# A hybrid decoder layer in float32 on TensorE: loads two tiles ahead, a fifth weight buffer, another place for the embedding's split

## The chip, the core and the metric

The kernel runs on one core of a Trainium2 chip. The metric is the device time of one execution in microseconds: the median of three runs of the kernel before, 2093.87 (2093.08 to 2097.32). All times of single instructions come from one further execution that the hardware profiler recorded.

## The reference

One layer of a decoder trunk in float32 on x of 1024 tokens x 2048 channels:

```python
h = rmsnorm(x, g_pre)
u = h @ w_in                     # 2048 x 7184, split into the heads' inputs and two gates
o_gla = rmsnorm(gla_chunked(...)) * silu(g_gate)    # 4 heads, gated linear attention
o_sb = stick_breaking(...) * silu(s_gate)           # 8 heads, stick-breaking attention
x = x + rmsnorm(concat(o_gla, o_sb) @ w_out, g_post)
x = x + sigmoid(x @ w_ple_gate + b) * (p @ w_ple_proj)
```

p has 256 channels for each token; `p @ w_ple_proj` is called the embedding here, and `w_p` is its weight.

## The kernel before

**Arithmetic.** A float32 operand is used as a sum of two rounded parts. `split(hi, lo, src)` makes them: ScalarE copies `src` into `hi` (L113), VectorE subtracts `hi` from `src` into `lo` (L114). A product in float32 is three matmuls for each 128 x 128 block of weight: hi with hi, lo with hi, hi with lo. Matmuls are 128 x 128 by 512 tokens; the tokens are in two halves (`hf` 0 and 1).

**Blocks.** The three big square products (gates, w_out, and w_g, which is `w_ple_gate`) are done in Strassen-Winograd form: seven products of half size instead of eight, with sums S1 to S4 of activations and differences of weights (b11, t1, t2, t3, t4). A stage is a loop over eight columns j of one or two products. A product is 24 matmuls into one `dn` bank. A stage with two products in a step loads three wide raw weights (`wload2`, 512 KB, 128 x 1024) in each step, takes differences of them on VectorE (`sub`, L876, `add`, L873), splits the results (`wsplit`) and, in the gates and w_out, stores two of the sums. Raw wide weights are in a pool `wr` of four buffers, the split ones in `wh` and `wl` of three each.

**The gates' S1 and S2.** They were summed from x earlier and stored in DRAM. `x_set` (L760) loads them a tile of 128 x 512 at a time (`u<-S2x_d`), and splits each (`ah<-u`, `al<-u`) into the activations of the gates' later stages. It is a generator that runs beside the small products of the gates (L818, L825; weights `raw`, `hi`, `lo`) and beside stick-breaking attention. That uses ScalarE for X<-z and E<-z (L592, L593), VectorE for a scan and copies, ScalarE again for X<-E (L333); later the rows come turned as `v`, split into `s`, and go to TensorE as t<-s,u.

**The embedding.** In three stages of w_g, products carry an `embed` between their matmuls: six matmuls with w_p into a bank z, t, z, o in turn. Its weight is loaded to `pr`, and split to `ph` and `pl` (128 x 256, one buffer each). Behind the product `gated` adds two banks (`ev<-dn,st`), ScalarE makes the sigmoid (`g<-ev,c`, L1203), VectorE multiplies it with the embedding (L1204, `ev<-t,g`).

**What sets the order.** The program is written in stages, and a scheduler puts the instructions of each engine into one list, by priority and by its own estimate of when operands are there. `tc.high_priority(offset=n)` draws the work inside it forward. `ahead` does so by 700 for wide loads and their splits, `soon` by 300 for what empties a bank; the embedding's load and split are drawn forward by 400. Each engine then works through its own list in order. The loads here are issued from SP's list.

The lines of the embedding before:

```python
wr, wh, wl = mt("pr", 1, 256), mt("ph", 1, 256, F32R), mt("pl", 1, 256, F32R)
with tc.high_priority(offset=400):
    dma2(wr, w_p[n])
    split(wh, wl, wr)
```

Of the kernel before, what the change touches and what calls it, by code (L numbers as in the profile page):

```python
# [12 lines left out]
F32R = mybir.dt.float32r  # L13
# [48 lines left out]
def layer(ctx, tc, xT, w_in, w_gate, w_lr, w_a2, b_a, g_pre, g_head, w_out, g_post,  # L62
# [4 lines left out]
    dma2 = nc.sync.dma_start  # L67
# [19 lines left out]
    def nm(base):  # L87
        serial[0] += 1
        return f"{base}_{serial[0]}"

    def ps(tag):
        bufs = {"dn": 4, "z": 2, "t": 1, "o": 1}[tag]
        return psum.tile([P, HT], F32, tag=tag, name=nm(tag), bufs=bufs)
# [6 lines left out]
    def mm(o, lhsT, rhs, start, stop):  # L100
        PE.matmul(o, lhsT, rhs, start=start, stop=stop)  # L101

    def f(t):
        return t.bitcast(F32)
# [7 lines left out]
    def split(hi, lo, src, eng=None):  # L112
        A.activation(hi, src, AF.Copy)  # L113
        (eng or V).tensor_tensor(lo, src, f(hi), op=ALU.subtract)  # L114
# [19 lines left out]
    def act_wide(hf, kp):  # L134
        return (act.tile([P, W], F32R, tag=f"h{hf}_{kp}", name=nm("ah")),
                act.tile([P, W], F32R, tag=f"l{hf}_{kp}", name=nm("al")))

    def part(t, k):
        return t[:, (k % 2) * HT:(k % 2 + 1) * HT]

    def parts(pairs):
        return [tuple(part(t, i) for t in pair) for pair in pairs for i in range(2)]
# [22 lines left out]
    pace = [0, PACE_QKV]  # L165

    def advance(queue):
        while queue:
            if next(queue[0], None) is not None:
                return True  # L170
            queue.popleft()
        return False
# [38 lines left out]
    pair = {}  # L211
# [3 lines left out]
    with tc.tile_pool(name="start", bufs=1) as sp:  # L215
# [21 lines left out]
        for q in range(4):  # L237
            w = [wload(w_in[n, q]) for n in range(2)]
            for kk in range(4):
                k = 4 * q + kk  # L240
                sl = slice(kk * P, (kk + 1) * P)
                for hf in HALVES:
                    raw = sp.tile([P, HT], F32, tag="xraw", name=nm("xraw"), bufs=20)
# [36 lines left out]
    with tc.tile_pool(name="att", bufs=1, reuse_waits="tile") as ap:  # L280
# [11 lines left out]
        def at(tag, shape=(P, HT), dt=F32):  # L292
            pool, bufs = (ap, BUFS[tag]) if tag in BUFS else (own[1], {**GLA_BUFS, **SB_BUFS}[tag])
            return pool.tile(list(shape), dt, tag=tag, name=nm(tag), bufs=bufs)
# [463 lines left out]
        g_sets = {"S1": [], "S2": []}  # L758

        def x_set(name, hf):  # L760
            for k in range(8):
                t = at("u")
                dma2(t, part(sx_d[name][k // 2], k))
                yield 1
                if k % 2 == 0:
                    wides = act_wide(hf, k // 2)
                pair = tuple(part(x, k) for x in wides)
                split(*pair, t)
                g_sets[name].append(pair)

        def small_product(a, src, evac):
            p = ps("dn")
            for q in range(2):
                hi, lo = wload(part(src, q))
                for kk in range(4):
                    k = 4 * q + kk
                    sl = slice(kk * P, (kk + 1) * P)
                    ah, al = a[k]
                    mm(p, hi[:, sl], ah, k == 0, False)
                    mm(p, lo[:, sl], ah, False, False)  # L780
                    mm(p, hi[:, sl], al, False, k == 7)
                    if k % 2:
                        step()
            with tc.high_priority(offset=300):
                evac(p)
# [22 lines left out]
        while beside:  # L808
            advance(beside)
        rate[1], pace[1] = RATE_TAIL, PACE_TAIL  # L810
        beside.append(x_set("S2", 1))
        for j in range(8):
            small_product(x_act[0][:8], w_gate[0, 0, j], keep_u1(j))
        while beside:
            advance(beside)
        beside.append(x_set("S1", 0))
        order_11 = (6, 7, 0, 1, 2, 3, 4, 5)
        for j in order_11[:8 - LAST_11]:  # L818
            small_product(x_act[0][8:], w_gate[1, 0, j], keep_11(j, lambda: at("u")))
# [9 lines left out]
    def mt(tag, bufs, n=W, dt=F32, name=None):  # L829
        pool = keep if tag == "ar" else mp if tag in ("wr", "wh", "wl", "cw") else late[0]  # L830
        return pool.tile([P, n], dt, tag=tag, name=nm(name or tag), bufs=bufs)
# [12 lines left out]
    if True:  # L844
# [31 lines left out]
            V.tensor_tensor(dst, a, b, op=ALU.subtract)  # L876

        def wload2(src):
            raw = mt("wr", 4)
            dma(raw, src)  # L880
            return raw

# [142 lines left out]
        for j in range(8):  # L1025
            with ahead():
                b11, t1, t2 = (wload2(w_gate[kh, nh, j]) for kh, nh in ((0, 0), (0, 1), (1, 1)))
                sub(t1, t1, b11)
                sub(t2, t1, t2)
                w2, w1 = wsplit(t2), wsplit(t1)  # L1030
                add(b11, b11, t2)
                dma2(t2_d[j], t2)
                dma2(t3_d[j], b11)
            p = product(g_sets["S2"], w2)
            with soon():
                add(u(j), p, part(u1_s[j // 2], j) if j < 6 else u(j))
            p = product(g_sets["S1"], w1)
            with soon():
                add(v(j), p, u(j))
# [5 lines left out]
        for j in range(8):  # L1045
            with ahead():
                t4, t2 = wload2(w_gate[1, 0, j]), wload2(t2_d[j])
                add(t4, t4, t2)
                w = wsplit(t4)
            p = product(x_act[1][8:], w)  # L1050
            with soon():
                add(u(j), p, u(j))
        drain()

        for j in range(8):
            with ahead():
                w = wsplit(wload2(t3_d[j]))
            p = product(sets["S3"], w)
            gate(j, 1, p, u(j))
            gate(8 + j, 1, p, v(j))  # L1060
# [110 lines left out]
        def load_p(hf):  # L1171
            raw = staged(pT[hf])
            hi, lo = mt("sq", 1, dt=F32R, name="ph"), mt("acc", 1, dt=F32R, name="pl")
            split(hi, lo, raw)
            p_act[hf] = parts([(hi, lo)])

        def embed(n, hf):
            def go():
                if hf not in p_act:
                    load_p(hf)  # L1180
                wr, wh, wl = mt("pr", 1, 256), mt("ph", 1, 256, F32R), mt("pl", 1, 256, F32R)
                with tc.high_priority(offset=400):
                    dma2(wr, w_p[n])
                    split(wh, wl, wr)
                z = ps(next(pw_tags))
                for k in range(2):
                    sl = slice(k * P, (k + 1) * P)
                    ah, al = p_act[hf][k]
                    mm(z, wh[:, sl], ah, k == 0, False)
                    mm(z, wl[:, sl], ah, False, False)  # L1190
                    mm(z, wh[:, sl], al, False, k == 1)
                pw[n, hf] = z
            return go

        def gated(n, hf, p, other, last=False):
# [43 lines left out]
        for j in range(8):  # L1239
            with ahead():  # L1240
                w = wsplit(wload2(w_g[1, 0, j]))
            p = product(sets[1], w, embed(j, 1))
            with soon():
                gated(j, 1, p, u(j))
# [29 lines left out]
        for j in range(8):  # L1274
            with ahead():
                w = wsplit(wload2(w_g[1, 1, j]))
            p = product(sets["S4"], w, embed(8 + j, 1))
            with soon():
                gated(8 + j, 1, p, v(j))
        drain()  # L1280

        for j in range(8):
            with ahead():
                t2, t3, t4 = wload2(t2_d[j]), wload2(w_g[0, 0, j]), wload2(w_g[1, 0, j])
                add(t3, t3, t2)
                add(t4, t4, t2)
                w3, w4 = wsplit(t3), wsplit(t4)
            p = product(sets["S3"], w3, embed(8 + j, 0), at=6 if j == 0 else 4)
            with soon():
                gated(8 + j, 0, p, v(j))  # L1290
                add(u(j), p, u(j))
            p = product(sets["A22"], w4, embed(j, 0))
            with soon():
                gated(j, 0, p, u(j), last=j >= 6)
# [74 lines left out]
```

## Time and profile before

| what | value |
|---|---|
| runs | 2093.87 us median of 3 (2093.08 to 2097.32) |
| profiled execution | 2095.95 us, of it 2094.3 span |
| TensorE busy | 2068.5 us of the span |
| VectorE, ScalarE, GpSimd busy | 1485.8, 876.8, 112.0 us |
| granted TensorE clock | 0.998 of full speed |

The span is from the first to the last instruction. The waits of an engine are the stretches in which it did nothing before an instruction, put down to what released it. A product's matmuls stand 0.227 us apart when nothing holds them up, a product takes 5.44 us and an embedding 1.36. Stages in question: S2's last tile is split at 1154 us; the gates' three-load stage runs from about 1190 to 1290, w_out's from 1440 to 1530; the embedding's first gated stage is around 1780 to 1840, the last stage from about 1980 to the end.

### The profile page before, as it was taken

Reading aid. Unit: us, or ns where it says so; the run is one execution under the profiler, and the core shown is the slowest. Engines: PE = TensorE matmul, PEld = TensorE weight load, DVE = VectorE, ACT = ScalarE, POOL = GpSimd, SP = SyncE. Lnnn points to the kernel's source line nnn. Section 1 sums busy time; section 2 is a strip of 40 time slices with the busy share of each in tenths; the row PEclk is TensorE's granted clock in tenths of the full one; section 3 lists DMA queues with packets and bytes.
Section 4 is the critical chain, followed back from the end, with each engine's and each line's share of the span. In section 5 each row is a group of like instructions: output and inputs, shape, how many; then the busy total and the mean of one; then the engine's idle time right before and its main releaser. Section 6 shows DMA issues by size and latency. Waiting matters only on the chain.

```text
span 2094.3 us, 26752 instructions
## 1 busy us (share of the span) xinstructions
PE 2068.5 (99%) x9712; PEld 1708.3 (82%) x9712; DVE 1485.8 (71%) x2243; ACT 876.8 (42%) x1390; POOL 112.0 (5%) x229
## 2 busy tenths in 40 slices
PE   9999999999999999999999999999999999999998
PEld 6788888888888888888887788888788888788887
DVE  8657777676767677666567667788778687876675
ACT  7333343333455455555456413344233444323332
POOL 4100000000011011101101000000000000000000
PEclk9999999999999999999999999999999999999999
DMA  6222222232244344433335788987977596886663
GB/s 217 68 71 72 86 72 86 66 89 63 82 105 107 94 102 118 107 92 101 80 89 145 220 289 281 317 308 274 339 284 269 166 320 229 295 279 214 229 206 107
DMA packets 229700, 352.81 MB, mean 168 GB/s; under 512 B 124336, under 2 KB 129344, under 8 KB 229568
## 3 DMA queue, kind: packets, MB, share of 16 engines
q1 hardware_dynamic: 228960, 349.00, 52.7%
q10 hardware_dynamic: 576, 2.10, 0.3%
q8 instruction: 76, 1.25, 0.2%
q14 instruction: 56, 0.46, 0.1%
q0 software_dynamic: 32, 0.01, 0.0%
HBM read 249.85 MB, written 73.92 MB: 155 GB/s over the span
## 4 chain that ended last, share of the span: by engine, by line
PE 76%; DMA 10%; DVE 9%; issue 3%; ACT 2%; POOL 0%; SPq 0%; DVEq 0%; ACTq 0%; POOLq 0%
PE dn L101 66%; PE z L101 5%; PE t L101 3%; PE o L101 2%; DVE wl L114 2%; DMA wr<-w_gate 2%; DMA wr<-w_g 2%; DMA E<-X 1%; DVE wr L876 1%; DVE wr L873 1%; DMA g_d<-wr 1%; DMA xraw<-xT 1%; DMA h_d<-st 1%; DMA wr<-w_out 1%; DMA ar<-og_d 0%
## 5 line engine op out<-in xcount | busy, mean ns | idle before, releaser
L101 PE MATMUL dn<-ah,hi 128*128 128x512 f32 x1408 | 562.7, 400 | 3.7 <-ACT u L736 1.4
L101 PE MATMUL dn<-ah,lo 128*128 128x512 f32 x1408 | 550.6, 391 | 0.2 <-DVE lo L114 0.2
L101 PE MATMUL dn<-al,hi 128*128 128x512 f32 x1408 | 550.3, 391 | 0.0
L101 PE MATMUL dn<-ah,wl 128*128 128x512 f32 x1216 | 474.0, 390 | 2.6 <-DVE wl L114 2.5
L101 PE MATMUL dn<-ah,wh 128*128 128x512 f32 x1216 | 473.5, 389 | 0.8 <-ACT wh L113 0.8
L101 PE MATMUL dn<-al,wh 128*128 128x512 f32 x1216 | 473.2, 389 | 0.0
L101 PEld LDWEIGHTS dn<-ah,hi 128*128 128x128 f32 x1408 | 265.6, 189 | 61.9 <-ACT ah L251 4.8
L101 PEld LDWEIGHTS dn<-al,hi 128*128 128x128 f32 x1408 | 264.9, 188 | 57.5 <-DVE al L252 0.3
L101 PEld LDWEIGHTS dn<-ah,lo 128*128 128x128 f32 x1408 | 265.7, 189 | 48.5 <-DVE lo L114 0.5
L113 ACT ACTIVATE wh<-wr 128x1024 fp32r<-128x1024 f32 x152 | 159.1, 1057 | 306.7 <-DVE wr L876 146.3
L101 PEld LDWEIGHTS dn<-ah,wl 128*128 128x128 f32 x1216 | 228.3, 188 | 52.1 <-DVE wl L114 5.1
L101 PEld LDWEIGHTS dn<-ah,wh 128*128 128x128 f32 x1216 | 228.3, 188 | 49.4 <-ACT wh L113 1.9
L101 PEld LDWEIGHTS dn<-al,wh 128*128 128x128 f32 x1216 | 228.3, 188 | 47.3
L114 DVE TENSOR_TENSOR wl<-wr,wh 128x1024 fp32r<-128x1024 f32 x152 | 185.2, 1219 | 6.6 <-ACT wh L113 6.5
L113 ACT ACTIVATE hi<-raw 128x512 fp32r<-128x512 f32 x192 | 119.8, 626 | 147.7 <-PE dn L101 138.9
L114 DVE TENSOR_TENSOR lo<-raw,hi 128x512 fp32r<-128x512 f32 x192 | 134.7, 703 | 57.3 <-ACT hi L113 57.1
L333 ACT ACTIVATE X<-E 128x256 uint16<-128x256 uint16 (+2 forms) x96 | 81.1, 844 | 128.3 <-DVE E L608 119.6
L603 DVE TENSOR_TENSOR_SCAN X<-X 128x128 f32<-128x128 f32 (+2 forms) x96 | 98.2, 1023 | 31.2 <-POOL X L597 21.3
L876 DVE TENSOR_TENSOR wr<-wr,wr 128x1024 f32<-128x1024 f32 x48 | 58.8, 1224 | 80.1 <-issue 23.7
L618 DVE COPY v<-E 128x512 uint16<-128x512 uint16 (+1 forms) x160 | 63.5, 429 | 56.9 <-DMA E<-X 47.9
L873 DVE TENSOR_TENSOR wr<-wr,wr 128x1024 f32<-128x1024 f32 x48 | 58.8, 1224 | 42.7 <-DMA wr<-w_g 29.5
L113 ACT ACTIVATE ah<-ar 128x1024 fp32r<-128x1024 f32 x46 | 48.5, 1061 | 85.5 <-DVE ar L873 35.1
(246 smaller groups left out, 2300.3 us busy)
## 6 DMA issues: line engine op xcount, KB each, us to landing
raw<-w_in SPq DMA_DIRECT2D x160, 256.0 KB, 2.7
wr<-w_g SPq DMA_DIRECT2D x64, 512.0 KB, 4.3
wr<-w_out SPq DMA_DIRECT2D x56, 512.0 KB, 5.1
wr<-w_gate SPq DMA_DIRECT2D x40, 512.0 KB, 5.5
g_d<-wr SPq DMA_DIRECT2D x32, 512.0 KB, 2.6
wr<-g_d SPq DMA_DIRECT2D x32, 512.0 KB, 4.9
ar<-h_d SPq DMA_DIRECT2D x28, 512.0 KB, 5.0
ar<-og_d SPq DMA_DIRECT2D x25, 512.0 KB, 5.4
```

The costliest lines, as they stand in the source:

```text
L101: PE.matmul(o, lhsT, rhs, start=start, stop=stop)
L113: A.activation(hi, src, AF.Copy)
L114: (eng or V).tensor_tensor(lo, src, f(hi), op=ALU.subtract)
L333: A.activation(pl.rearrange("p (two n) -> p two n", two=2), src.bitcast(U16)[:, :2 * n].rearrange("p (n two) -> p two n", two=2), AF.Copy)
L603: V.tensor_tensor_scan(rev, rev, rev, initial=kq[:, n:n + 1], op0=ALU.mult, op1=ALU.bypass)
L618: V.tensor_copy(to[:, :, :m, j], w[:, :, 2 * g:2 * g + m])
L873: V.tensor_tensor(dst, a, b, op=ALU.add)
L876: V.tensor_tensor(dst, a, b, op=ALU.subtract)
```

## The change

Three parts. `x_set` loads a tile two steps before it splits it, and does the first two loads at the start. `pace[1] = 2`: while S1's set is filled, the generators in `beside` move on at every second call of `step` instead of every fourth (`PACE_TAIL`). The pool `wr` has five buffers. The embedding's weight is loaded and split by `prepare`, which `embed` calls for the following embedding behind its own six matmuls: the load is drawn forward by 100, the split stands at the priority of that place. The order of embeddings over all stages is listed in `turns`. The DMA scratch is halved.

```diff
@@ -758,15 +758,22 @@
         g_sets = {"S1": [], "S2": []}
 
         def x_set(name, hf):
-            for k in range(8):
+            def load(k):
                 t = at("u")
                 dma2(t, part(sx_d[name][k // 2], k))
-                yield 1
+                return t
+
+            ahead_2 = [load(0), load(1)]
+            yield 1
+            for k in range(8):
                 if k % 2 == 0:
                     wides = act_wide(hf, k // 2)
                 pair = tuple(part(x, k) for x in wides)
-                split(*pair, t)
+                split(*pair, ahead_2.pop(0))
                 g_sets[name].append(pair)
+                if k + 2 < 8:
+                    ahead_2.append(load(k + 2))
+                yield 1
 
         def small_product(a, src, evac):
             p = ps("dn")
@@ -814,6 +821,7 @@
         while beside:
             advance(beside)
         beside.append(x_set("S1", 0))
+        pace[1] = 2
         order_11 = (6, 7, 0, 1, 2, 3, 4, 5)
         for j in order_11[:8 - LAST_11]:
             small_product(x_act[0][8:], w_gate[1, 0, j], keep_11(j, lambda: at("u")))
@@ -876,7 +884,7 @@
             V.tensor_tensor(dst, a, b, op=ALU.subtract)
 
         def wload2(src):
-            raw = mt("wr", 4)
+            raw = mt("wr", 5)
             dma(raw, src)
             return raw
 
@@ -1174,14 +1182,24 @@
             split(hi, lo, raw)
             p_act[hf] = parts([(hi, lo)])
 
+        turns = [(j, 1) for j in range(16)] + [(n, 0) for j in range(8) for n in (8 + j, j)]
+        w_ready = {}
+
+        def prepare(i):
+            if i < len(turns) and turns[i] not in w_ready:
+                wr, wh, wl = mt("pr", 1, 256), mt("ph", 1, 256, F32R), mt("pl", 1, 256, F32R)
+                with tc.high_priority(offset=100):
+                    dma2(wr, w_p[turns[i][0]])
+                split(wh, wl, wr)
+                w_ready[turns[i]] = wh, wl
+
         def embed(n, hf):
             def go():
                 if hf not in p_act:
                     load_p(hf)
-                wr, wh, wl = mt("pr", 1, 256), mt("ph", 1, 256, F32R), mt("pl", 1, 256, F32R)
-                with tc.high_priority(offset=400):
-                    dma2(wr, w_p[n])
-                    split(wh, wl, wr)
+                i = turns.index((n, hf))
+                prepare(i)
+                wh, wl = w_ready[n, hf]
                 z = ps(next(pw_tags))
                 for k in range(2):
                     sl = slice(k * P, (k + 1) * P)
@@ -1190,6 +1208,7 @@
                     mm(z, wl[:, sl], ah, False, False)
                     mm(z, wh[:, sl], al, False, k == 1)
                 pw[n, hf] = z
+                prepare(i + 1)
             return go
 
         def gated(n, hf, p, other, last=False):
@@ -1356,7 +1375,7 @@
                                   j[:, None] % 32 >= 16], axis=1).astype(np.float32),
     }
     nc = bacc.Bacc("TRN2", target_bir_lowering=False, num_devices=1,
-                   dynamic_dma_scratch_size=1024)
+                   dynamic_dma_scratch_size=512)
     args = {n: nc.dram_tensor(n, a.shape, mybir.dt.from_np(a.dtype), kind="ExternalInput").ap()
             for n, a in ins.items()}
     out = nc.dram_tensor("out", (2, KP, P, W), F32, kind="ExternalOutput").ap()
```

**ScalarE, last split of S2.** Before: rows of stick-breaking (X, E, hi, s, u) and, fourth in the list, the split `ah` of the last S2 tile; numbers behind the names count the tiles.

```order
L797 ACTIVATE u_10985<-dn_10882 128x512
L113 ACTIVATE s_11011<-v_11008 128x512
L113 ACTIVATE hi_11150<-raw_11149 128x512
L113 ACTIVATE ah_11069<-u_11073 128x512
L592 ACTIVATE X_11025<-z_11021 128x512
L593 ACTIVATE E_11026<-z_11021 128x512
L333 ACTIVATE X_11032<-E_11026 128x1024
L113 ACTIVATE hi_11175<-raw_11174 128x512
```

After, the same split (now from another `u`, as `ah_11071<-u_10985`) stands here:

```order
L113 ACTIVATE ah_10877<-u_10808 128x512
L113 ACTIVATE hi_10829<-raw_10828 128x512
L113 ACTIVATE ah_11071<-u_10881 128x512
L592 ACTIVATE X_10667<-z_10657 128x128
L593 ACTIVATE E_10668<-z_10657 128x128
L113 ACTIVATE ah_11071<-u_10985 128x512
L333 ACTIVATE X_10680<-E_10668 128x256
```

The last split of S2 has moved 37 rows up on ScalarE, from behind `hi_11150` to before X<-E of an earlier group; X<-z of the old place is now directly behind `hi`.

**ScalarE and VectorE, third and fourth embedding of the first gated stage.** `ph` and `pl` are the halves of the embedding's weight, `g` the sigmoid, `ev` the gate, `wl` the low half of a wide weight. ScalarE before:

```order
L113 ACTIVATE ah_15588<-ar_15578 128x1024
L113 ACTIVATE wh_15948<-wr_15946 128x1024
L1203 ACT_TABLE_LOAD
L1203 ACTIVATE g_15834<-ev_15830,c_611 128x512
L113 ACTIVATE ph_15918<-pr_15917 128x256
L113 ACTIVATE wh_15998<-wr_15996 128x1024
L1203 ACTIVATE g_15890<-ev_15830,c_611 128x512
L113 ACTIVATE ph_15969<-pr_15968 128x256
```

ScalarE after:

```order
L113 ACTIVATE wh_15954<-wr_15952 128x1024
L1222 ACT_TABLE_LOAD
L1222 ACTIVATE g_15840<-ev_15836,c_611 128x512
L113 ACTIVATE wh_16004<-wr_16002 128x1024
L1222 ACTIVATE g_15896<-ev_15836,c_611 128x512
L113 ACTIVATE ph_15877<-pr_15876 128x256
L113 ACTIVATE ah_15888<-st_13175 128x1024
L113 ACTIVATE wh_16055<-wr_16053 128x1024
L113 ACTIVATE ah_15642<-ar_15632 128x1024
L113 ACTIVATE ph_15931<-pr_15930 128x256
```

The split of the third embedding (`ph_15918` before, `ph_15877` after) stood ahead of the second `wh` and of `g_15890`, and stands behind `g_15896` now; that of the fourth (`ph_15969`, now `ph_15931`) stands behind three more rows. VectorE before, with both splits (`pl_15919`, `pl_15970`):

```order
L988 SCALAR_TENSOR_TENSOR ar_15606<-ar_15606,c_609,rstd_15423 128x512
L114 TENSOR_TENSOR pl_15919<-pr_15917,ph_15918 128x256
L988 SCALAR_TENSOR_TENSOR ar_15606<-ar_15606,c_609,rstd_15423 128x512
L873 TENSOR_TENSOR st_13175<-st_13175,cw_15620 128x1024
L873 TENSOR_TENSOR ev_15830<-dn_15843,st_13168 128x512
L114 TENSOR_TENSOR wl_15999<-wr_15996,wh_15998 128x1024
L1204 TENSOR_TENSOR ev_15830<-t_15869,g_15890 128x512
L873 TENSOR_TENSOR ar_15606<-ar_15606,ar_15608 128x1024
L114 TENSOR_TENSOR pl_15970<-pr_15968,ph_15969 128x256
L873 TENSOR_TENSOR st_13175<-st_13175,ar_15606 128x1024
```

VectorE after, around the third embedding's `pl_15878`:

```order
L881 TENSOR_TENSOR st_13175<-st_13175,cw_15620 128x1024
L881 TENSOR_TENSOR ev_15836<-dn_15849,st_13168 128x512
L881 TENSOR_TENSOR ar_15606<-ar_15606,ar_15608 128x1024
L114 TENSOR_TENSOR wl_16005<-wr_16002,wh_16004 128x1024
L1223 TENSOR_TENSOR ev_15836<-t_15869,g_15896 128x512
L114 TENSOR_TENSOR pl_15878<-pr_15876,ph_15877 128x256
```

That `pl` has moved behind a sum `ar`, `wl` and the multiplication ev<-t. Two rows further down, VectorE goes on to the fourth embedding's `pl_15932`:

```order
L884 TENSOR_TENSOR ar_15632<-ar_15632,st_13175 128x1024
L884 TENSOR_TENSOR wr_16218<-wr_16218,wr_16216 128x1024
L114 TENSOR_TENSOR wl_16056<-wr_16053,wh_16055 128x1024
L881 TENSOR_TENSOR ev_15836<-ev_15836,ar_15837 128x1024
L881 TENSOR_TENSOR ev_15945<-dn_15907,st_13169 128x512
L114 TENSOR_TENSOR al_15643<-ar_15632,ah_15642 128x1024
L884 TENSOR_TENSOR wr_16220<-wr_16218,wr_16220 128x1024
L114 TENSOR_TENSOR wl_16106<-wr_16103,wh_16105 128x1024
L1223 TENSOR_TENSOR ev_15945<-z_15923,g_15949 128x512
L881 TENSOR_TENSOR ev_15945<-dn_15958,st_13169 128x512
L114 TENSOR_TENSOR al_15889<-st_13175,ah_15888 128x1024
L114 TENSOR_TENSOR pl_15932<-pr_15930,ph_15931 128x256
```

The fourth's `pl`, which stood one row behind a sum `ar`, now stands behind two differences wr<-wr of the next stage's weights, two `wl`, two `al` and two `ev`. On TensorE the first matmul with `ph` of the fourth embedding has 30 other matmuls behind it before the first with `pl`; before there were none.

**VectorE, last stage.** `o` and `z` are embeddings' banks, `wr<-wr,wr` sums of weights for a following step. Before:

```order
L873 TENSOR_TENSOR ev_17364<-dn_17432,st_13168 128x512
L114 TENSOR_TENSOR wl_17592<-wr_17585,wh_17591 128x1024
L1204 TENSOR_TENSOR ev_17364<-o_17454,g_17471 128x512
L873 TENSOR_TENSOR ev_17364<-ev_17364,cw_17365 128x1024
L114 TENSOR_TENSOR pl_17556<-pr_17554,ph_17555 128x256
L873 TENSOR_TENSOR wr_17692<-wr_17692,wr_17688 128x1024
L873 TENSOR_TENSOR ev_17530<-dn_17492,st_16207 128x512
L873 TENSOR_TENSOR st_13169<-dn_17492,st_13169 128x512
```

After:

```order
L1223 TENSOR_TENSOR ev_17370<-o_17454,g_17477 128x512
L881 TENSOR_TENSOR ev_17370<-ev_17370,cw_17371 128x1024
L881 TENSOR_TENSOR wr_17803<-wr_17803,wr_17801 128x1024
L881 TENSOR_TENSOR ev_17536<-dn_17498,st_16213 128x512
L881 TENSOR_TENSOR st_13169<-dn_17498,st_13169 128x512
L114 TENSOR_TENSOR wl_17602<-wr_17593,wh_17601 128x1024
L1223 TENSOR_TENSOR ev_17536<-z_17514,g_17540 128x512
L114 TENSOR_TENSOR pl_17523<-pr_17521,ph_17522 128x256
L881 TENSOR_TENSOR wr_17805<-wr_17805,wr_17801 128x1024
```

The embedding's `pl` (`pl_17556` before, `pl_17523` after) stood ahead of a sum `wr`, two evacuations and `wl`; it now stands behind them and behind ev<-z.

## Rows read from the trace of the kernel before

**Rows 1.** The page's first part: busy us, share of the span, instructions, by engine:

```profile
PE 2068.5 (99%) x9712; PEld 1708.3 (82%) x9712; DVE 1485.8 (71%) x2243; ACT 876.8 (42%) x1390; POOL 112.0 (5%) x229
```

**Rows 2.** TensorE's waits: engine, line, releaser: us in total, times, longest:

```profile
PE dn L101 <- DVE wl L114: 2.5, 4, 0.8
PE t L101 <- ACT s L113: 2.5, 1, 2.5
...
PE t L101 <- DVE pl L114: 1.7, 2, 1.0
...
PE o L101 <- DVE pl L114: 1.3, 1, 1.3
PE dn L101 <- ACT hi L113: 1.2, 1, 1.2
...
PE dn L101 <- ACT wh L113: 0.8, 2, 0.4
```

**Rows 3.** Timeline, ScalarE, S2's last split: start, us, instruction, [idle before <- releaser]:

```profile
1154.52 0.63 ACT L113 ACTIVATE ah<-u 128x512 fp32r<-128x512 f32 x1 [3.06 <-DMA u<-S2x_d]
1155.06 0.58 ACT L592 ACTIVATE X<-z 128x512 f32<-128x512 f32 x1
...
1157.90 1.06 ACT L333 ACTIVATE X<-E 128x1024 uint16<-128x1024 uint16 x1 [1.78 <-DVE E L608]
1158.87 0.61 ACT L113 ACTIVATE hi<-raw 128x512 fp32r<-128x512 f32 x1
...
1163.56 0.61 ACT L113 ACTIVATE s<-v 128x512 fp32r<-128x512 f32 x1
```

**Rows 4.** Timeline, TensorE, the same stretch:

```profile
1159.53 0.50 PE L101 MATMUL dn<-ah,hi 128*128 128x512 f32 x1 [1.23 <-ACT hi L113]
...
1164.23 1.31 PE L101 MATMUL t<-s,u 128*128 128x256 f32 x3 [2.52 <-ACT s L113]
```

**Rows 5.** The page's DMA issues: operation, queue, count, KB, us to landing:

```profile
wr<-w_gate SPq DMA_DIRECT2D x40, 512.0 KB, 5.5
g_d<-wr SPq DMA_DIRECT2D x32, 512.0 KB, 2.6
```

**Rows 6.** Timeline, VectorE, gates' three-load stage: differences of a step:

```profile
1255.91 2.49 DVE L876 TENSOR_TENSOR wr<-wr,wr 128x1024 f32<-128x1024 f32 x2 [4.83 <-DMA wr<-w_gate]
```

**Rows 7.** Windows, w_out's stage: us, engines' busy, PEclk, DMA share, GB/s:

```profile
1465.00:1500.00 35.00, 32.66 (x140) 25.94 (x139) 27.19 (x26) 11.39 (x13) 0.00 (x0) 1.00 0.95 346
```

**Rows 8.** Timeline, VectorE, w_out's stage:

```profile
1479.47 1.22 DVE L114 TENSOR_TENSOR wl<-wr,wh 128x1024 fp32r<-128x1024 f32 x1
```

**Rows 9.** Timeline, ScalarE, first gated stage:

```profile
1797.57 0.72 ACT L1203 ACTIVATE g<-ev,c 128x512 f32<-128x512 f32 x1 [3.19 <-DVE ev L873]
```

**Rows 10.** Timeline, TensorE, third and fourth embedding:

```profile
1796.14 0.39 PE L101 MATMUL z<-ph,ph 128*128 128x512 f32 x1
...
1802.94 0.39 PE L101 MATMUL o<-ph,ph 128*128 128x512 f32 x1
```

**Rows 11.** Timeline, VectorE, third embedding:

```profile
1796.79 0.68 DVE L873 TENSOR_TENSOR ev<-dn,st 128x512 f32<-128x512 f32 x1
1797.39 1.22 DVE L114 TENSOR_TENSOR wl<-wr,wh 128x1024 fp32r<-128x1024 f32 x1
1798.53 0.68 DVE L1204 TENSOR_TENSOR ev<-t,g 128x512 f32<-128x512 f32 x1
1799.13 1.22 DVE L873 TENSOR_TENSOR ar<-ar,ar 128x1024 f32<-128x1024 f32 x1
```

**Rows 12.** DMA issues between 1780 and 1830 us, as in rows 5:

```profile
wr<-w_g SPq DMA_DIRECT2D x9, 512.0 KB, 4.9
```

**Rows 13.** Timeline, VectorE, last stage:

```profile
2014.84 1.23 DVE L873 TENSOR_TENSOR wr<-wr,wr 128x1024 f32<-128x1024 f32 x1 [1.29 <-DMA wr<-w_g]
```

**Rows 14.** Timeline, TensorE, last stage, the embedding at that place:

```profile
2016.51 0.39 PE L101 MATMUL t<-ph,ph 128*128 128x512 f32 x1
```

**Rows 15.** VectorE's waits, columns as in rows 2:

```profile
DVE wr L873 <- DMA wr<-w_g: 29.5, 14, 3.1
```

## Prediction

> **What bounds the kernel now.** The page's first part comes first [rows 1]: TensorE is busy 2068.5 of 2094.3 us, VectorE 71%, ScalarE 42%. So TensorE is the bound, and the change adds and removes no matmul of weight: it can only touch the 25.8 us in which TensorE stands idle. The list of TensorE's waits [rows 2] splits that by releaser, and the reader looks for the names that the diff moves. `hi` and `s` (1.2 + 2.5) sit behind S2's last split on ScalarE; `wl` and `wh` (2.5 + 0.8) are the wide weights; `pl` (1.7 + 1.3) is the embedding's weight. Together 10.0 us, 0.5% of the time: that is the ceiling, if nothing is pushed out elsewhere. Such a row shows a little less than a stall costs, since a stalled matmul also starts slower; from start to start I find 0.2 to 0.4 us more for each, and give terms in that measure.
>
> The profiled execution took 2095.95 us, 2.08 above the median of 2093.87. The sum is made against the profiled one, and its difference is taken over to the median. Two medians of this kernel can be told apart from about 0.2%, 4.2 us.
>
> **Part a: S1 and S2 loaded two tiles ahead.** In the trace ScalarE idles 3.06 us for the load of S2's last tile, at 1151.46 to 1154.52 [rows 3]. Behind that split stand X<-z (1155.06), X<-E (1157.90), the `hi` that TensorE waits 1.23 for and the `s` that it waits 2.52 for [rows 3, 4]. In the new order that split stands 37 rows further up. X<-z can then start 3.6 us earlier, at 1151.46. What follows doesn't get all of it: X<-E waits for VectorE's `E`, and VectorE has its own queue of scans between. I put X<-E at 1155.7, 2.2 earlier. Then `hi` starts at 1156.7, before TensorE wants it, and `s` 4.69 later as now (1163.56 - 1158.87), at 1161.4 instead of 1163.56. The start of TensorE's t (1164.23) moves by the same **2.2 us**. Bounds: 0.5, if VectorE's queue gives back next to nothing, and 3.7, both waits whole. The added work is none: the same sixteen loads and splits. S1's splits move up on ScalarE too, 0.63 each; the idle time of 42% busy ScalarE covers them, and without that cover one costs 0.63.
>
> **Part b: the fifth buffer for wide weights.** In the stages with three loads in a step a step lasts two products, 2 x 24 matmuls at 0.227, 10.9 us. One buffer's turn is the difference on VectorE (2.49 for two, 1.23 for one), the store of it (2.6) and the next load into it (5.5) [rows 5, 6]: 9.3 us without queueing, so with four buffers the load lands late (VectorE idles 4.83 for it), and with five it is issued a load earlier. In the gates I take both stalls as gone: **1.4 us** (0 to 1.4). In w_out's stage the same stalls come to 3.2 from start to start, but there the DMA engines are at 0.95 in the stretch of the stalls [rows 7], and an earlier issue doesn't make a full queue faster. Also the two differences of the next step, which wait for these loads, now stand ahead of the `wl` of the running step in VectorE's queue, at the place where `wl` (1479.47) comes last today [rows 8]. I leave 1.7 us of stall: a gain of **1.5 us**, between -1.5 (the differences wait for two loads, and `wl` behind them) and 3.2. In single-load stages the splits have 4 to 8 us to spare; the fifth buffer costs nothing there.
>
> **Part c: the embedding's split behind the last use of its buffer.** Before, ph and pl are drawn forward with a high priority and mostly stand early; the price is six matmuls' wait at three places, 3.0 us by [rows 2], two of them (2.6 from start to start) at embeddings that the change reaches. Afterwards they are written behind the previous embedding, at the priority of the place, and so they stand behind work that waits for something else.
>
> The third embedding of the first gated stage: its ph stands behind g on ScalarE, and g waits for VectorE's ev. g starts at 1797.57 and takes 0.72 [rows 9], so ph is there at about 1798.4; TensorE wants it at 1796.14 [rows 10]: 2.2 late. Its pl stands behind ev, ar, wl and ev<-t [rows 11]: 1796.79 plus these four at their spacing (0.6, 1.1, 1.1, 0.6) plus its own 0.42 is 1800.6, where TensorE, moved by 2.2 and with four matmuls of the product between, wants it at 1799.5: 0.9 more. Together 3.1. The fourth: pl stands behind two differences of the next stage's weights, each of which waits for a load of 4.9 us [rows 12]: 1799.4 + 4.9 + 1.2 + 4.9 + 1.2 gives 1812.1, and behind them wl, two ev and al (3.8) to 1816.1. TensorE reaches the first ph matmul at 1802.94 + 3.1 [rows 10] and, since the order puts 30 other matmuls (6.8 us) ahead of pl's, wants pl about 1814: 2.1 late. In the same way I get 0.8, 1.0, 0 and 0.4 for the next four, each from its place in the new order and the times of the same rows. Sum 7.4, against 2.6 that goes: **-4.8 us**. Lower end 0 (each ev and each load earlier by what TensorE is late), upper end 7.4.
>
> The last stage, with two embeddings in a step: pl, which stands ahead of the sum wr<-wr,wr (2014.84) today [rows 13], stands behind it, two evacuations, wl and ev. From 2014.84 that is 3.5 to 4.1 us at the spacing above, so pl is there at about 2018.3 if the fifth buffer brings the load half a microsecond forward; TensorE wants it at 2016.5 [rows 14]: 1.8 late. At two more places (near 1989 and 2044) the order is the same and I get 1.1 and 1.0: **-3.9 us**. The upper end lies at 10: the sums of this line waited 29.5 us at 14 places, 2.1 each [rows 15], and three more such waits can fall in front. The lower end is 0.
>
> The Trainium skill says in "PSUM — Partial Sum Buffer", section "Engine vs sequencer instructions", that the queues of ScalarE and VectorE are strictly first in, first out. By it no 0.4-us split gets past what waits ahead of it; if a queue let it pass, part c would cost nothing and the sum would be that of the fast rival below. The trace agrees so far: ScalarE's X<-z starts only behind the split that idled 3.06 [rows 3].
>
> The sum: 2.2 + 1.4 + 1.5 - 4.8 - 3.9 = -3.6, so **3.6 us slower**: 2099.6 for the profiled execution, about 2097.6 for the median.
>
> **Rivals.** *Change does what it says* (fast): loads and VectorE's work come early enough that the splits, though behind other work, are never late. Then parts a and b give 5.1, and c between 0 and 2.6: 1.3 in the middle, 2087.5. For it speaks that fewer transfers stall VectorE with five buffers, and VectorE idles 29% of the time; against it that TensorE, at 0.99, reaches the third embedding 2.2 before g is done, whoever loads when. It decides if g ends before 1796. The Trainium skill's "Trainium Kernel Development and Optimization", section "Best Practices", asks to overlap transfers with compute by double buffers; by that rule a and b are gains and 5.1 or more is what the time falls by. [rows 3] show such an idle stretch for a load, and agree for part a; no run here shows it yet for a buffer.
>
> *Only the embedding stage pays* (same): its VectorE is busiest, and in the last stage the split still lands in time. 2.2 + 1.4 + 1.5 - 4.8 = +0.3, about 2093.6.
>
> *VectorE's in-order differences become the bound* (slow): in w_out's stage and the next two-load stage the differences stand ahead of wl by a whole step and wait for loads that the full DMA queue brings late. Place: VectorE's L876 rows of w_out; price: b's second half at -1.5 instead of +1.5, 2.4 at the two-load stage behind the gates, 1.5 more in the last stage. 3.6 + 3.0 + 2.4 + 1.5 = 10.5, about 2104. It decides if a difference there waits more than 5 us with wl behind it. For it: DMA at 0.95 [rows 7]. Against: five buffers shorten just these loads.
>
> **How the numbers follow.** Forecast (both embedding stages pay, 2095 to 2101) 0.50; fast 0.20; same 0.15; slow 0.15. The forecast's centre, 2097.6, lies close to the line of 0.2% at 2098.1, so half of it counts as no change and half as slower. Faster 0.20, same 0.25 + 0.15 = 0.40, slower 0.25 + 0.15 = 0.40. The range of 8 in 10 leaves out half of the fast and a half of the slow case at their far ends: 2088 to 2104.
>
> **What would show it.** Part a: ScalarE's 3.06 for u<-S2x_d gone, TensorE's waits for `hi` and `s` down from 3.7 to about 1.5. Part b: VectorE's idle time for wr<-w_gate down, TensorE's waits for `wl` and `wh` at half of 3.3. Part c: new waits of TensorE for `ph` (some 2 us at the third embedding) and `pl` at z, t and o in both embedding stages, 9 to 11 us together against 3.0. The forecast is wrong if the sum for `ph` and `pl` stays under 5 us (then the time falls), or if `wl` grows past 5 us (then the slow case holds).

## Result, and the profile after

The changed kernel takes 2098.98 us in the median of 22 runs (2094.71 to 2102.08), the kernel before 2093.57 in as many runs beside it. The ratio is 1.002, with a 95% interval of 1.0013 to 1.0027: slower by some 4.2 us (the two medians lie 5.4 apart; the ratio is the better measure, and 4.2 is used below). The profiled execution of after took 2097.77 us, its span 2096.1.

TensorE's work is the same as in [rows 1]; first the page's first part, then TensorE's waits of after, in the columns of [rows 2]:

```profile
PE 2068.0 (99%) x9712; PEld 1708.0 (81%) x9712; DVE 1485.1 (71%) x2243; ACT 876.5 (42%) x1390; POOL 111.9 (5%) x229
```

```profile
PE t L101 <- ACT ph L113: 3.1, 4, 1.3
PE t L101 <- DVE pl L114: 3.0, 2, 2.3
PE z L101 <- ACT ph L113: 2.9, 1, 2.9
...
PE t L101 <- ACT s L113: 1.3, 1, 1.3
...
PE z L101 <- DVE pl L114: 0.9, 1, 0.9
PE o L101 <- ACT ph L113: 0.6, 2, 0.5
PE dn L101 <- ACT hi L113: 0.4, 1, 0.4
PE o L101 <- DVE pl L114: 0.3, 1, 0.3
```

The reader is to see three things. `wl` and `wh`, 3.3 us before, are gone from the list. `hi` and `s` fell from 3.7 to 1.7. `ph` and `pl`, 3.3 before, come to 10.8.

Where that lies is read by counting TensorE's matmuls in both traces (9712 in each) and taking the difference of the start of the same number:

| stretch, by the times of before | after minus before, us |
|---|---|
| up to 1139 | -1.8 |
| 1139 to 1172, S2's last split | -3.3 |
| 1172 to 1336, the gates' stages with three and two loads | -2.4 |
| 1336 to 1558, the stages up to the end of w_out's three loads | -3.8 |
| 1558 to 1843, to the end of the first gated stage | +5.6 |
| 1843 to the end | +7.4 |

So 11.2 us were won and 13.0 lost; the span grew by 1.8. (The kernel's own executions differ by some 10 us between the lowest and the highest, so a single pair of traces shows places, and the ratios of the runs show sizes.)

### The profile page after: what moved, and what is told of

It reads as the page before. It is cut to its first block, busy times and chain, and to the rows that moved or that the text cites. A ratio compares the mean times of both kernels' runs of the same rounds, so it can differ in the third digit from the quotient of the medians.

```text
span 2096.1 us, 26737 instructions
## 1 busy us (share of the span) xinstructions
PE 2068.0 (99%) x9712; PEld 1708.0 (81%) x9712; DVE 1485.1 (71%) x2243; ACT 876.5 (42%) x1390; POOL 111.9 (5%) x229
```

## Experiments

All ratios are to the kernel before, run on the same chip beside it, with 95% intervals.

### Each part by itself: e1_ab, e2_c, e3_a, e4_b

e1_ab is the changed kernel with the embedding as before:

```diff
-                i = turns.index((n, hf))
-                prepare(i)
-                wh, wl = w_ready[n, hf]
+                wr, wh, wl = mt("pr", 1, 256), mt("ph", 1, 256, F32R), mt("pl", 1, 256, F32R)
+                with tc.high_priority(offset=400):
+                    dma2(wr, w_p[n])
+                    split(wh, wl, wr)
```

> The changed kernel with the embedding as before: S1 and S2 loaded ahead and five wide buffers. Theory 1 (the parts add up): in the two traces TensorE of the changed kernel is 11.2 us ahead of the kernel before when w_out's stage is over, so this gains about 11 us: some 2082.5, ratio 0.9947. The terms of the prediction (2.2 + 2.9) would give 2088.5, ratio 0.9976. Theory 2 (part of the 11 us is chance of one execution): between these two. TensorE's waits for ph and pl stay near the 3.3 us of the kernel before.

Measured: 2091.10 us, ratio 0.9991 (0.9978 to 1.0003). Every expected gain was too large. In its trace 10.3 us were won by 1494 us, as in after, but most of that was lost again further on, with the embedding as before: TensorE's waits for `ph` and `pl` are 8.4 us, not near 3.3.

e2_c is the kernel before with `turns`, `prepare` and the new `embed` alone.

> The kernel before with the embedding's weight prepared behind the previous embedding, all else as before (four wide buffers). Theory 1: TensorE lost 13 us to the embedding's weight in the changed kernel, of it 5.5 in the first gated stage and 7.3 in the last, and loses it here too: 2106.5, ratio 1.0062. Theory 2: the cost comes from the fifth buffer, whose loads and differences stand ahead of the embedding's in SP's and VectorE's lists; without it at most 5 us are lost: 2098, ratio 1.002. By the prediction's own terms, 8.7: 2102, ratio 1.0042.

Measured: 2100.91 us, ratio 1.004 (1.0024 to 1.0055), 8.4 us slower: near the prediction's own term of 8.7, and between the two theories, whose ratios both lie outside the interval (1.0062, and 1.002 at most). The part costs without a fifth buffer too.

e3_a is the kernel before with the new `x_set` and its pace; e4_b the kernel before with one number changed (and the DMA scratch, to make room):

```diff
-            raw = mt("wr", 4)
+            raw = mt("wr", 5)
```

> The kernel before with S1 and S2 loaded two tiles ahead, nothing else. The traces show 5.0 us up to the start of the gates' three-load stage, of which 1.8 were gained before the place of S2's last split. If all of that comes from this part: 2088.5, ratio 0.9976. If the prediction's term is right: 2.2, ratio 0.9989.

> The kernel before with five wide buffers, nothing else. By the traces 2.2 us in the gates' stages and 3.8 in w_out's: 6.1 in all, 2087.5, ratio 0.9971; the prediction's terms give 2.9, ratio 0.9986. If the fifth buffer's differences delay the embedding's split in VectorE's list (theory 2), a part of it is lost again in the gated stages: ratio 0.998 to 1.000, with TensorE's waits for pl above 3.0 us.

Measured: e3_a 1.0006 (0.9994 to 1.0019), e4_b 1.0017 (1.0004 to 1.003). Both lie above every ratio that was expected. By themselves, neither gains, and the fifth buffer loses. (`x_set` and its pace were not run apart, nor was the smaller scratch without the buffer. The profiled executions, 2098.15 and 2101.26 us, were the slowest of twelve each, so their traces show places and overstate sizes.) TensorE's waits of e3_a between 1190 and 1530 us, where [rows 2] have 2.5 and 0.8:

```profile
PE dn L101 <- DVE wl L114: 4.4, 6, 1.1
PE dn L101 <- ACT wh L113: 1.7, 2, 1.6
```

TensorE came to these stages 3.6 us earlier and the wide loads did not: VectorE's waits for wr<-w_gate there are 23.5 us, before 23.4. By 1503 us the lead was gone. In e4_b the same count of matmuls shows 1.6 us won between 1172 and 1558 us, and then this happened in the first gated stage, on VectorE and, in the second fence, on TensorE:

```profile
1830.67 1.23 DVE L876 TENSOR_TENSOR wr<-wr,wr 128x1024 f32<-128x1024 f32 x1 [2.62 <-DMA wr<-w_g]
1831.82 0.42 DVE L114 TENSOR_TENSOR pl<-pr,ph 128x256 fp32r<-128x256 f32 x1
```

```profile
1828.43 0.39 PE L101 MATMUL o<-ph,ph 128*128 128x512 f32 x1
1832.29 0.50 PE L101 MATMUL o<-ph,pl 128*128 128x512 f32 x1 [3.47 <-DVE pl L114]
```

A difference of wide weights for the following stage waits 2.62 us for its load, `pl` stands behind it, and TensorE stands 3.47 us. `pl` had long been ready: TensorE's use of `ph` at 1828.43 shows that `ph` was there. Counted from the start this is the 69th difference of weights and the ninth `pl`. With four buffers that `pl` stood behind the 68th, which did not wait, and ahead of the 69th (1840.31). VectorE before:

```profile
1831.49 1.22 DVE L876 TENSOR_TENSOR wr<-wr,wr 128x1024 f32<-128x1024 f32 x1
1832.63 0.42 DVE L114 TENSOR_TENSOR pl<-pr,ph 128x256 fp32r<-128x256 f32 x1
```

The sum of e4_b's waits for `ph` and `pl` is 11.3 us against 3.3: more than in the changed kernel.

### The embedding's place against the differences: e5_ab_700, e9_700 to e12_abc_700

```diff
-                with tc.high_priority(offset=400):
+                with tc.high_priority(offset=700):
                     dma2(wr, w_p[n])
                     split(wh, wl, wr)
```

e5_ab_700 is e1_ab with this line.

> The kernel of e1_ab (S1 and S2 ahead, five wide buffers, embedding as before) with the embedding's load and split drawn forward by 700 instead of 400, so that its pl stands ahead of the next difference of wide weights in VectorE's list and not behind it. Theory A (the fifth buffer draws the differences ahead of pl, and pl then waits for a wide load): TensorE's waits for ph and pl fall from 8.4 us in e1_ab to about 3, the time to some 2086, ratio 0.9965. Rival B (the embedding's load itself is late, whatever the order on VectorE): waits stay at 7 to 9 us, ratio 0.999 as e1_ab.

Measured: 2084.75 us, ratio 0.9945 (0.9929 to 0.9961). The ninth `pl` and the 69th difference again, now in e5_ab_700:

```profile
1822.34 0.42 DVE L114 TENSOR_TENSOR pl<-pr,ph 128x256 fp32r<-128x256 f32 x1
1823.81 1.23 DVE L884 TENSOR_TENSOR wr<-wr,wr 128x1024 f32<-128x1024 f32 x1 [1.05 <-DMA wr<-w_g]
```

and its waits of TensorE for the embedding:

```profile
PE z L101 <- DVE pl L114: 2.5, 2, 1.4
...
PE o L101 <- DVE pl L114: 1.3, 1, 1.3
...
PE t L101 <- DVE pl L114: 0.4, 1, 0.4
```

`pl` stands one row ahead of the difference, the waits are 4.2 us, half of e1_ab's 8.4, and 9.6 us come back by the ratios (0.9945 against 0.9991), 6.6 by the spans of the two profiled executions (2084.7 against 2091.3): theory A, with more time gained and less wait removed than expected (2086, and 3 us left). The line moves the load too, so by itself it doesn't rule out theory B. The trace of e1_ab parts them: its ninth `ph` was split at 1818.78 and its `pl` only at 1825.51, directly behind the 69th difference, so there the order on VectorE held it. B has a smaller part: in the last stage of e1_ab `ph` waits 3.03 us for its load, and TensorE 1.2 us for `ph`. The four kernels below put the same line into the kernel before (e9_700), with five buffers (e10_b_700), with S1 and S2 ahead (e11_a_700), and into `prepare` of the changed kernel, load and split (e12_abc_700).

> The kernel before with the embedding's load and split drawn forward by 700 instead of 400, nothing else. With four wide buffers only a part of the differences stands ahead of pl, so at most the 3.3 us of TensorE's waits for ph and pl can go: ratio 0.9985 to 1.000. If the ten us of e5_ab_700 come from this line alone: ratio 0.995.

> e9_700 with five wide buffers. Theory A (the fifth buffer gains in the three-load stages and e4_b lost it at the embedding): against e4_b (ratio 1.0017, waits for ph and pl 11.3 us) the waits fall to 4 or so and the time by 7 us: ratio 0.998. If e4_b was slow for another reason: ratio stays over 1.000.

> e9_700 with S1 and S2 loaded two tiles ahead and four wide buffers. In e3_a the 3.6 us gained at S2's last split were given back by 1500 us, at waits for wl and wh (6.1 us in the three-load stages against 3.3 before): TensorE came earlier, the loads did not. If that holds, ratio as e9_700 within 0.001. If parts a and b simply add: 0.0025 less than e9_700.

> The changed kernel with the load and the split of the embedding's weight both drawn forward by 700: written behind the previous embedding as in the change, but ahead of the differences. Theories A and C together: what cost the change its gain was the embedding's late load and its place behind the differences, not where prepare is called; ratio 0.9945 as e5_ab_700. If preparing one embedding earlier has a cost of its own: 0.997 or more.

Measured, with the two rows above them for comparison:

| parts | embedding's offset 400 | offset 700 |
|---|---|---|
| neither | 1 (before) | 1.0002 (0.9990 to 1.0014) |
| a, loads ahead | 1.0006 (0.9994 to 1.0019) | 1.0005 (0.9994 to 1.0016) |
| b, five buffers | 1.0017 (1.0004 to 1.0030) | 0.9981 (0.9971 to 0.9990) |
| a and b | 0.9991 (0.9978 to 1.0003) | 0.9945 (0.9929 to 0.9961) |
| a, b and prepared one embedding earlier | 1.002 as changed (load 100, split in place) | 0.9958 (0.9945 to 0.9970) |

The line alone does nothing that can be told from noise: it has an effect only where there are five buffers. b then gains 4 us, as theory A expected (0.998). a gains nothing with four buffers and some 7.5 us with five (the intervals leave 4 us either way). In the trace of e11_a_700 TensorE is 5.1 us ahead of e9_700 at 1172 us and 0.5 at 1558, and it waits 6.5 us in all for `wl` (e9_700: 3.9): with four buffers the lead of TensorE is waited away. VectorE's waits for wr<-w_gate between 1190 and 1530 us show the same: 22 to 24 us in every kernel with four buffers, 17.7 and 19.8 with b alone (e4_b, e10_b_700), 8.8 to 9.1 with a and b (after, e1_ab, e5_ab_700). That a needs b was what e11_a_700 was to tell; how much a is worth with b was not foreseen. Of preparing the weight one embedding earlier no effect can be told once it is drawn ahead of the differences: the intervals of the two last rows overlap, and 0.9958 lies between what was expected without a cost (0.9945) and with one (0.997). e5_ab_700 and e12_abc_700 beat both kernels, with medians of 2084.75 and 2084.29 us.

### The load or the split of part c: e6_load_early, e7_split_early, e8_c_pr2

The changed kernel, with one of the two drawn forward by 400; e6_load_early:

```diff
-                with tc.high_priority(offset=100):
+                with tc.high_priority(offset=400):
                     dma2(wr, w_p[turns[i][0]])
                 split(wh, wl, wr)
```

> The changed kernel with the embedding's load drawn forward by 400 instead of 100; its split stays at the place of the change. In SP's list the third embedding's load stands ahead of two loads of x and three others that it stood behind. Theory C (the split waits for a late load in SP's list): ScalarE's wait of ph for the load falls from 38.9 us by a half or so, TensorE's waits for ph and pl from 10.8 us to about 7, ratio 1.0005. Rival D (the split's own place in the lists of ScalarE and VectorE, as the prediction has it): waits stay near 10 us, ratio 1.002 as the changed kernel.

e7_split_early:

```diff
                 with tc.high_priority(offset=100):
                     dma2(wr, w_p[turns[i][0]])
-                split(wh, wl, wr)
+                with tc.high_priority(offset=400):
+                    split(wh, wl, wr)
```

> The changed kernel with the embedding's split drawn forward by 400, its load at 100 as in the change. Rival D (the split's place): TensorE's waits for ph and pl fall from 10.8 us to 8 (that of e1_ab), ratio near 0.999 to 1.000. Theory C (the load): the split stands further ahead and still waits for the load, now with other work behind it: waits stay at 10 us or grow, ratio 1.002 or more.

e8_c_pr2 is e2_c with `mt("pr", 2, 256)`.

> The kernel of e2_c (before, with only the embedding's part) and two buffers for the embedding's raw weight: its load starts one embedding earlier, while the split stays where e2_c has it. Theory C (load): e2_c's loss of 8.4 us goes down to 3 or less, ratio 1.0015 or lower, and ScalarE's wait of ph for the load (23.5 us) nearly goes. Rival D (the split's place): ratio stays near 1.004.

Measured: e6_load_early 0.9988 (0.9976 to 1.0001), e7_split_early 1.0015 (1.0004 to 1.0026), e8_c_pr2 1.0011 (0.9998 to 1.0023) against e2_c's 1.004. An earlier load takes back all that part c cost on top of a and b (e1_ab: 0.9991), an earlier split nothing that can be told from the changed kernel's 1.002: theory C, for the sum. (TensorE's waits for `ph` and `pl` moved less than the ratio: 8.4 us in e6_load_early, where 7 were expected, 12.2 in e7_split_early, 10.8 in the changed kernel.) ScalarE's waits of `ph` for the load are 38.9 us in the changed kernel, 21.1 in e6_load_early, 35.2 in e7_split_early.

Not for the third embedding, though. In e6_load_early its `ph` is early (ScalarE, 1783.87, ahead of g), and VectorE and TensorE still go:

```profile
1789.03 1.22 DVE L114 TENSOR_TENSOR wl<-wr,wh 128x1024 fp32r<-128x1024 f32 x1
1790.16 0.69 DVE L1223 TENSOR_TENSOR ev<-t,g 128x512 f32<-128x512 f32 x1
1790.76 0.42 DVE L114 TENSOR_TENSOR pl<-pr,ph 128x256 fp32r<-128x256 f32 x1
```

```profile
1787.02 0.39 PE L101 MATMUL z<-ph,ph 128*128 128x512 f32 x1
...
1791.24 0.50 PE L101 MATMUL z<-ph,pl 128*128 128x512 f32 x1 [2.92 <-DVE pl L114]
```

There `pl` waits behind `wl` and ev<-t for nothing that it needs, and TensorE stands 2.92 us: as in e8_c_pr2 (2.96). So the split's place costs 3 us at this one embedding, and the late load the rest, most of it in the last stage: by the count of matmuls against before, after loses 7.4 us there and e6_load_early 3.2, e2_c 3.2 and e8_c_pr2 none.

## Why the prediction was right, and where it was wrong

The forecast, 3.6 us slower, stands beside 4.2 by the ratio. The way and the sum were right, the sum by luck: its terms were off in both directions and cancelled. By the ratios, a and b together gained 1.9 us instead of 5.1 (e1_ab, between 4.6 gained and 0.6 lost), and c cost 6.1 on top of them instead of 8.7.

**Part a: the step held, the sum's additivity did not.** It put X<-E and the start of t 2.2 us earlier. ScalarE of after, beside [rows 3], and TensorE, beside [rows 4]:

```profile
1149.62 0.58 ACT L592 ACTIVATE X<-z 128x512 f32<-128x512 f32 x1
...
1153.94 1.06 ACT L333 ACTIVATE X<-E 128x1024 uint16<-128x1024 uint16 x1 [3.26 <-DVE E L608]
...
1159.51 0.61 ACT L113 ACTIVATE s<-v 128x512 fp32r<-128x512 f32 x1
```

```profile
1160.17 0.50 PE L101 MATMUL t<-s,u 128*128 128x256 f32 x2 [1.30 <-ACT s L113]
```

The 3.06 us behind the load are gone; X<-E came at 1153.94 instead of 1157.90, 4.0 earlier, of which 1.8 were there before this stretch: 2.2. ScalarE's idle time before X<-E grew from 1.78 to 3.26: VectorE's `E` sets it, as forecast. `t` moved by 4.1, 2.3 without the 1.8. The whole stretch gives 3.3, 1.1 more than the term; some 0.7 of that is TensorE's clock, of which the last section tells. Alone, though, a is worth nothing (e3_a, e11_a_700). It can only be kept where the next bound, the wide loads, moves too. The prediction added a and b and did not ask for this.

**Part b, its gain: the way was right, the size stays open.** 2.9 were forecast. The two traces show 6.2 between 1172 and 1558 us, and no wait for `wl` or `wh` is left. But 3.8 of that lie behind 1336 us, in the stages with w_out, and there e9_700 and e8_c_pr2, with four buffers, are 3.1 us faster than the trace of before too, and e2_c 1.1: that trace was slow at this place, so the 3.8 are not shown to be the buffer's. By the ratios b gains 4.4 where the embedding is out of the way (1.0002 to 0.9981, some 3 us either way). The 1.7 us of stall that I left in w_out's stage, because the next step's differences stand ahead of `wl` there, did not show in after: they do stand there, but TensorE waits for no `wl`. VectorE's waits for wr<-w_out between 1190 and 1530 us fell from 15.0 us to 11.2, but are 8.7 in e8_c_pr2 with four buffers; those for wr<-w_gate fell from 23.4 to 9.1, for which a was needed too.

**Part b, its cost: left out.** "The fifth buffer costs nothing there" was said of single-load stages. It is the step that failed most. The fifth buffer lets the following step's or stage's difference be issued, and listed, ahead of `pl`, in the gated stages too, and that wait stops everything behind it on VectorE. e4_b shows it: 8 us more of waits for the embedding with c not in it, in a slow execution, and 3.6 us lost by the ratio where 2.9 were to be gained. I had put such a place at "the fourth" and in the last stage, but under part c. The runs take the one in the last stage from c: e1_ab, without c, still waits 2.1 us for a `pl` there, and e2_c, with c alone, does not.

**Part c: right in sum at the third embedding, too large at the fourth, another cause in the last stage.** The third was worked out as 3.1 us, 2.2 for `ph` and 0.9 for `pl`. After, TensorE, and ScalarE:

```profile
1785.12 0.39 PE L101 MATMUL dn<-al,wh 128*128 128x512 f32 x1
1788.39 0.50 PE L101 MATMUL z<-ph,ph 128*128 128x512 f32 x1 [2.88 <-ACT ph L113]
```

```profile
1786.42 0.72 ACT L1222 ACTIVATE g<-ev,c 128x512 f32<-128x512 f32 x1 [3.16 <-DVE ev L881]
...
1787.92 0.42 ACT L113 ACTIVATE ph<-pr 128x256 fp32r<-128x256 f32 x1 [0.78 <-DMA pr<-w_p]
```

From 1785.12 to 1788.39 it is 3.04 beyond a matmul's 0.23, all of it for `ph`; `pl` was there at 1789.52, and TensorE, which took it at 1789.93, did not wait. So 3.1 came out by luck here too: `ph` was 0.8 later than forecast, and the 0.9 for `pl` never came. The forecast had left out the 0.42 that `ph` itself takes. `ph` stood behind g, as said (g ends 1787.14), and then 0.78 more for its load, which I had not reckoned. SP's rows:

```profile
1781.56 0.33 SPq L888 DMA_DIRECT2D wr<-w_g  x1
1782.69 0.33 SPq L870 DMA_DIRECT2D ar<-h_d  x1
1783.07 0.42 SPq L1192 DMA_DIRECT2D pr<-w_p  x1
```

SP had issued that load at 1783.07, though its buffer was free with the end of the second `pl` at 1778.56: with its priority down from 400 to 100 it stood in SP's list behind a wide load, which SP could issue only at 1781.56, and a load of h. That the load too was moved, and past what, the prediction didn't price: that step is missing in it. Behind the wait some 1.4 us more went at half clock (last section).

The fourth embedding, forecast at 2.1, waited 0.5 for `ph` and 0.3 for `pl`: `pl` came behind the two differences, as forecast, but the first didn't wait for its load and the second only 0.72 us, where I had put 4.9 for each, one behind the other. The sum itself was off too, by less: 1799.4 + 4.9 + 1.2 + 4.9 + 1.2 is 1811.6 and not 1812.1, TensorE's 1802.94 + 3.1 + 6.8 is 1812.8 and not 1814, and at the third embedding 1800.6 less 1799.5 is 1.1 and not 0.9.

In the last stage 3.9 were forecast and 5.2 are in the list, at four places. The largest is the mechanism that was forecast, though the fifth buffer brings it and not c. After on VectorE and TensorE:

```profile
1983.17 1.22 DVE L881 TENSOR_TENSOR wr<-wr,wr 128x1024 f32<-128x1024 f32 x1 [2.46 <-DMA wr<-w_g]
...
1987.24 0.41 DVE L114 TENSOR_TENSOR pl<-pr,ph 128x256 fp32r<-128x256 f32 x1
```

```profile
1985.00 0.40 PE L101 MATMUL dn<-ah,wh 128*128 128x512 f32 x1
1987.71 0.80 PE L101 MATMUL t<-ph,pl 128*128 128x512 f32 x1 [2.31 <-DVE pl L114]
```

That is [rows 13] again: a sum that waits for its load, and `pl` behind it. At two of the others TensorE waits for `ph`, and `ph` for its load: 21.8 us of ScalarE's time in this stage, against 8.8 in e6_load_early.

**The rivals.** The fast one failed at its own condition: g ended at 1787.14, TensorE wanted `ph`, which stands behind it, at 1785.3. The slow one's mechanism, differences that hold up VectorE in order, is real, but not where I put it (w_out, [rows 7]): it acts at the embedding. What the Trainium skill says in "PSUM — Partial Sum Buffer", section "Engine vs sequencer instructions", of strictly ordered queues is what e4_b's rows show, with 3.47 us beside it. What the Trainium skill says in "Trainium Kernel Development and Optimization", section "Best Practices", of overlapping loads with compute was borne out by a and b together once the embedding stood ahead of the differences (0.9945), and not by a or b alone with the embedding as it was (1.0006, 1.0017).

## What to carry to other kernels

A deeper buffer doesn't only bring loads forward: it brings forward the instructions that wait for those loads, and on an engine that works in order they go ahead of short work that had been ready; so look for what is small and urgent behind each of them, and give it the higher priority. A stall that is removed is kept only if the next thing that TensorE waits for moves too, so test two such edits together as well as apart. And when a diff lowers a priority, price the load and the computation apart: here the load was the dear one.

## What was not expected of the hardware

A wait of TensorE can cost more than its length. After the 2.52 us of [rows 4], the granted clock of the kernel before was at half (1.2 GHz of 2.4) for several microseconds, and then came back. Windows of before: us, busy time of PE, PEld, DVE, ACT, POOL, granted clock, DMA share, GB/s:

```profile
1162.00:1164.20 2.20, 0.00 (x0) 0.00 (x0) 1.17 (x2) 1.57 (x2) 0.00 (x0) 0.94 0.75 237
1164.20:1170.00 5.80, 5.77 (x16) 4.68 (x17) 4.24 (x9) 2.71 (x5) 0.00 (x0) 0.50 0.96 238
```

The same after the 2.31 us of the last stage in after:

```profile
1985.00:1987.70 2.70, 0.40 (x2) 0.00 (x0) 2.66 (x4) 0.72 (x1) 0.00 (x0) 0.92 0.07 21
1987.70:1990.00 2.30, 2.29 (x5) 1.82 (x6) 0.34 (x1) 0.00 (x0) 0.00 (x0) 0.50 0.73 262
```

Summed over the matmuls with spacings near twice 0.227, such stretches cost 2.5 us in before and 4.2 in after (1.8 at S2's split, 1.4 at the third embedding, 1.0 here). It did not follow every long wait: behind the 3.47 us of e4_b it stayed at 1.00:

```profile
1832.30:1834.00 1.70, 1.70 (x7) 1.41 (x8) 1.70 (x3) 0.72 (x1) 0.00 (x0) 1.00 0.59 200
```

What decides it, the runs here don't show.
